# Attention of a two-layer backbone: TensorE order written out, values in groups of six row blocks, VectorE sums three blocks per instruction

## The chip, the cores and the metric

The kernel runs on one core of a Trainium2 chip. The metric is the device time of one execution in microseconds (us). A core has five engines with instruction queues of their own: TensorE (PE; its weight loads are shown apart as PEld), VectorE (DVE), ScalarE (ACT), GpSimd (POOL) and SyncE (SP, here only an issuer of DMAs). Each runs its instructions in the order in which they were put into its queue and waits on semaphores for the others. SBUF is the on-chip memory, PSUM the eight banks into which TensorE writes (a bank holds 512 float32 in each of 128 partitions).

## The reference

Two pre-norm layers over 256 context and 2048 latent tokens, width 1024: multi-head latent attention, then bidirectional gated linear attention. The change is in the softmax attention of the first: 16 heads, 64 plain and 32 rotary numbers a head. Context queries see the 256 context keys, latent queries all 2304.

```python
def one_block(qi):
    s = jnp.einsum('bqhrd,bkhd->bhrqk', qi, k, preferred_element_type=F32) * scale
    p = jax.nn.softmax(s, axis=-1).astype(v.dtype)
    return jnp.einsum('bhrqk,bkhe->bqhre', p, v)
...
oc = attention_blocks(qc, kc, vc)
ox = attention_blocks(qx, jnp.concatenate([kc, kx], axis=1), jnp.concatenate([vc, vx], axis=1))
...
out(o, gate) = (o.reshape(b, n, MLA_WIDTH) * jax.nn.silu(gate)) @ w_out
```

## The kernel before

**Tiling.** The heads are handled in eight pairs. A pair has five *steps*: one of 256 context queries over two key blocks, and four of 512 latent queries over 18 key blocks of 128. A key block of a step is an *item*: 32 × 18 + 8 × 2 = 592, of which 16 are half as wide, 584 in full ones. For an item TensorE makes the scores of both heads (`st`, L603): ten matmuls, five terms in split float32, head 0 in TensorE's row groups of the upper 64 rows and head 1 in the lower 64, which run side by side. ScalarE takes the exponential (`pe`, L605) into one of eight buffers. TensorE multiplies `pe` with the values (`po`, L625, one PSUM bank for a step, four matmuls an item).

**Sums.** The denominator is the sum of the 18 `pe` tiles of a step over blocks and then over keys. VectorE adds the even blocks and the last two into `acc0` (L610 the first pair, L612 the rest), GpSimd the other odd ones into `acc1`; at the end of the step VectorE adds the two (L615), and two pairs of matmuls with ones sum over the keys (L637, `finish`). ScalarE takes the reciprocal by Ln and Exp (L640, L641), GpSimd multiplies the output with its gate (L639) and VectorE with the reciprocal (L643).

**Maxima.** The softmax needs a row maximum, which goes as one more row into the queries of a step. So for each step, ahead of it, TensorE computes approximate scores with queries in the partitions (L484, a *set* of four matmuls: two heads, two terms, 128 queries by 512 keys, the fifth stretch of keys only 256), each head into one of three PSUM banks `pmx`, and VectorE reduces each bank to a maximum (L486). A large step has 4 × 5 = 20 sets, a context step 2. A set needs two of the three banks, so its second bank is one that the set before it used, and is free only when VectorE has reduced that. At the end of a step's maxima (L489 to L495) a small reduce, a transpose on TensorE, a negation and two DMAs put them into the queries. The same three banks serve L637 and the modulation of later layers (L72, L82, L93).

**Order.** A loop over items writes: due sets of maxima (`rate`, about one an item), a modulation part every 20 items, the scores of an item, and after every third block of a step the values of these three (L625). The framework's scheduler then lays each engine's queue out by its own estimate of times; only what is pinned (`keep_in_program_order`) stays as written. In the attention stage nothing on TensorE is pinned.

Of the kernel before, what the change touches and what calls it, by code (L numbers as in the profile page):

```python
# [19 lines left out]
P = 128  # L20
# [44 lines left out]
def modulation_block(k, layer, nb, w, wp, ps, pt, gT, shT, ng, I, sel, condT, gates, gbc_d, bufs, tag="mod_s", bias=None):  # L65


    nc = k.nc
    cs = slice(nb * 512, nb * 512 + 512)
    for i in range(2):  # L70
        for r in range(4):
            nc.tensor.matmul(ps[32 * r:32 * r + 32, :512], condT[:, 4 * i + r, :], w[4 * i + r], start=(i == 0), stop=(i == 1))  # L72
    yield
    if bias is None:
        bias = wp.tile([2, 512], F32, name="mod_b", tag="mod_b", bufs=bufs)
        nc.sync.dma_start(bias, I["ada_b"][layer:layer + 1, cs].to_broadcast([2, 512]))
    m = wp.tile([P, 512], F32, name="mod_s", tag=tag, bufs=bufs)
    nc.scalar.copy(m, ps[:, :512])
    nc.vector.tensor_tensor(m[0:2, :], m[0:2, :], bias, op=ALU.add)
    if nb < 4:  # L80
        for kk in range(4):
            nc.tensor.matmul(pt[:, 2 * kk:2 * kk + 2], m[:, kk * P:kk * P + P], sel[:, 0:2 * P:P], start=True, stop=True)  # L82
        k0 = (nb % 2) * 4
        dst = (shT if nb < 2 else gT)[:, k0:k0 + 4, :]
        src = pt[:, :8].rearrange("p (k c) -> p k c", c=2)
        if nb < 2:
            nc.vector.tensor_copy(dst, src)
        else:
            nc.vector.tensor_scalar(dst, src, 1.0, None, op0=ALU.add)
            nc.vector.tensor_tensor(dst, dst, ng[:, k0:k0 + 4].unsqueeze(2).to_broadcast([P, 4, 2]), op=ALU.mult)  # L90
    else:
        for j in range(gates):
            nc.tensor.matmul(pt, sel[:, j * P:j * P + P], m, start=True, stop=True)  # L93
# [24 lines left out]
def body(ctx, tc, I, out, stop=99, dbg=None):  # L118
# [321 lines left out]
    def load_q(si):  # L440
# [8 lines left out]
        def put():  # L449
            qs = qsp.tile([P, 2, 2, 512], F32R, name="qs", tag="qs")  # L450
# [14 lines left out]

    def maxima():

        for si, (pr, ci) in enumerate(steps):
            c0, n = CHUNKS[ci]
# [6 lines left out]
            for t in range(nq):  # L476
                for b in range(npart):
# [3 lines left out]
                    for i, kk in enumerate((kh, kr[0])):  # L481
                        for j in range(2):
                            js = slice(64 * j, 64 * j + 64)
                            nc.tensor.matmul(ps[j][:, :w], qs[js, 0, i, t * P:t * P + P], kk[js, bs], start=(i == 0), stop=(i == 1))  # L484
                    for j in range(2):
                        nc.vector.reduce_max(mx[:, j * nq + t, b:b + 1], ps[j][:, :w], axis=AX.X)  # L486
                    yield
            mc = qsp.tile([P, 8], F32, name="mc", bufs=2)
            nc.vector.reduce_max(mc[:, :2 * nq], mx[:, :2 * nq, :npart], axis=AX.X)  # L489
            pt = pmp.tile([P, 512], F32, name="pmx")  # L490
            nc.tensor.transpose(pt[:2 * nq, :P], mc[:, :2 * nq], ident)
            mr = qsp.tile([8, P], F32R, name="mr", bufs=2)
            nc.vector.tensor_scalar(mr[:2 * nq, :], pt[:2 * nq, :P], -1.0, None, op0=ALU.mult)
            for j in range(2):
                nc.sync.dma_start(qs[64 * j + 32:64 * j + 33, 1, 1, :n].bitcast(F32), mr[j * nq:j * nq + nq, :].bitcast(F32))  # L495
            yield

    stream = maxima()
    fed, lead, due = 0, 36, 0.0
    with pool("p2q", 2) as sp, pool("ps2q", 5, space=PSUM) as psp:  # L500
# [20 lines left out]
        def feed():  # L521
            nonlocal fed, due
            due += 0.82
            while fed < min(due, lead):
                fed += 1
                next(stream, None)

# [51 lines left out]
    with pool("p3", 2) as sp, pool("ps3", 2, space=PSUM) as psp:  # L579
# [5 lines left out]

        def scores(si, kt, nk):
            pr, ci = steps[si]
            c0, n = CHUNKS[ci]
            kh, kl = kb[pr % 2]
            qs = qss[si]  # L590
            if kt == 0:
                gt = sp.tile([P, 512], F32, name="gt")
                nc.sync.dma_start(gt[:, :n], gate_d[pr, :, c0:c0 + n])
                acc = [sp.tile([P, 2, 512], F32, name=f"acc{e}", tag=f"acc{e}", bufs=1) for e in range(2)]
                live[si] = dict(gt=gt, acc=acc, seen=[[], []], pe={})
            st_ = live[si]
# [3 lines left out]
            for i, (a, s, r, m) in enumerate(terms):  # L600
                for j in range(2):
                    js = slice(64 * j, 64 * j + m)
                    nc.tensor.matmul(st[:, j, :n], a[js, ks], qs[js, s, r, :n], start=(i == 0), stop=(i == len(terms) - 1))  # L603
            pe = sp.tile([P, 2, 512], F32, name="pe", bufs=8)
            nc.scalar.activation(pe[:, :, :n], st[:, :, :n], AF.Exp, scale=SCALE)  # L605
            st_["pe"][kt] = pe
            e = 1 if kt % 2 == 1 and 2 < nk and kt < nk - 2 else 0
            seen, acc, eng = st_["seen"][e], st_["acc"][e], (nc.vector, nc.gpsimd)[e]
            if len(seen) == 1:
                eng.tensor_tensor(acc[:, :, :n], seen[0][:, :, :n], pe[:, :, :n], op=ALU.add)  # L610
            elif len(seen) > 1:
                eng.tensor_tensor(acc[:, :, :n], acc[:, :, :n], pe[:, :, :n], op=ALU.add)  # L612
            seen.append(pe)
            if kt == nk - 1 and st_["seen"][1]:
                nc.vector.tensor_tensor(st_["acc"][0][:, :, :n], st_["acc"][0][:, :, :n], st_["acc"][1][:, :, :n], op=ALU.add)  # L615

        def values(si, kt, nk):
# [5 lines left out]
            po, pe, vt = st_["po"], st_["pe"][kt], vts[pr]  # L623
            for j in range(2):
                nc.tensor.matmul(po[64 * j:64 * j + 64, :n], vt[:, kt, 64 * j:64 * j + 64], pe[:, j, :n], start=(kt == 0), stop=(kt == nk - 1))  # L625
            if kt == nk - 1:
                st_["ob"] = sp.tile([P, 512], F32, name="ob")
                nc.scalar.copy(st_["ob"][:, :n], po[:, :n])

        def finish(si):  # L630
            pr, ci = steps[si]
            c0, n = CHUNKS[ci]
            st_ = live.pop(si)
            acc, ob = st_["acc"][0], st_["ob"]
            pss = pmp.tile([P, 512], F32, name="pmx")
            for j in range(2):
                nc.tensor.matmul(pss[64 * j:64 * j + 64, :n], ones[:, 0:64], acc[:, j, :n], start=True, stop=True)  # L637
            rs = sp.tile([P, 512], F32, name="rs", bufs=1)
            nc.gpsimd.tensor_tensor(ob[:, :n], ob[:, :n], st_["gt"][:, :n], op=ALU.mult)  # L639
            nc.scalar.activation(rs[:, :n], pss[:, :n], AF.Ln)  # L640
            nc.scalar.activation(rs[:, :n], rs[:, :n], AF.Exp, scale=-1.0)  # L641
            yield
            nc.vector.tensor_tensor(ob[:, :n], ob[:, :n], rs[:, :n], op=ALU.mult)  # L643
            (nc.scalar if si == len(steps) - 1 else nc.sync).dma_start(o_d[ci][pr, :, :], ob[:, :n])

        def mods():

            for layer, nb in [(0, 4), (0, 5)] + [(1, nb) for nb in range(6)]:
                w = modulation_load(k, layer, nb, sp)
                yield  # L650
                pm = [pmp.tile([P, 512], F32, name="pmx") for _ in range(2)]
                for _ in modulation_block(k, layer, nb, w, sp, pm[0], pm[1], gT[layer], shT[layer], ng[layer], I, sel, condT, 2 - layer, gbc_d[layer], 1):
                    pass
# [11 lines left out]
        def first_y(oh, ol):  # L665
# [7 lines left out]
            y0 = sp.tile([P, 2, 512], F32, name="y0", tag="pe", bufs=8)  # L673
# [25 lines left out]
        total = sum(21 if ci else 3 for _, ci in steps)  # L699
        rate = total / len(items)  # L700
        fed0 = fed
        done = []
        extra = mods()
        nv = 0
        for i in range(len(items) + 2):
            if i < len(items):
                si, kt, nk = items[i]
                if steps[si][1] == 1 and kt == 6 and steps[si][0] + 1 < NPAIR:
                    tasks += [(load_k, (steps[si][0] + 1, c)) for c in range(len(CHUNKS))]
                    load_v(steps[si][0] + 1)  # L710
                if kt == 0:
                    if si + 3 < len(steps):
                        tasks.insert(sum(f is load_q for f, _ in tasks), (load_q, (si + 3,)))
                if i % 3 == 1:
                    fetch(1)
                while fed < min(lead, fed0 + 0.1 * i) + rate * (i + 1):
                    fed += 1
                    next(stream, None)
                if i > 40 and i % 20 == 10 and i < len(items) - 80:
                    next(extra, None)  # L720
                scores(si, kt, nk)
                if i == len(items) - 70:
                    raw = out_load(0)
                if i == len(items) - 60:
                    out_weights(0, raw)
                if i == len(items) - 40:
                    raw = out_load(1)
                if i == len(items) - 30:
                    o0 = first_o()
            if i >= 2 and (items[i - 2][1] % 3 == 2 or items[i - 2][1] == items[i - 2][2] - 1):  # L730
                for si, kt, nk in items[nv:i - 1]:
                    values(si, kt, nk)
                    if kt == nk - 1:
                        done += [(i + 1 + u, g) for g in [finish(si)] for u in range(2)]
                nv = i - 1
            if i == len(items) + 1:
                out_weights(1, raw)
                first_y(*o0)
            while done and (done[0][0] <= i or i == len(items) + 1):
                next(done.pop(0)[1], None)  # L740
# [744 lines left out]
```

## Time and profile before

| | |
|---|---|
| median of 3 runs | 3941.18 us (3940.01 to 3943.34) |
| the profiled execution | 3936.72 us, span 3934.7 us |
| TensorE busy over the span | 3716.6 us, 94% |
| VectorE, ScalarE, GpSimd busy | 2404.2, 1357.8, 1133.0 us |
| granted TensorE clock, mean of the span | 0.973 of full speed |
| attention stage | 693 to 2559 us of the span |

A matmul of the trace is busy from its start to its modelled end, and consecutive ones overlap, so start-to-start distances tell more than durations. "Idle before" of a group is the time its engine stood still ahead of it, with the instruction that ended it. The granted clock is the share of TensorE's full clock that the throttle gave in a stretch.

### The profile page before, as it was taken

How to read it: one execution, taken by the hardware profiler on the slowest of the kernel's cores; microseconds unless marked ns; L12 is line 12 of the kernel's file. 1: busy time of each engine (PE TensorE's matmuls, PEld its weight loads, DVE VectorE, ACT ScalarE, POOL GpSimd, SP SyncE). 2: the span in 40 equal slices, each digit the busy share in tenths (PEclk: the TensorE clock that was granted, in tenths of full speed). 3: DMA queues.
4: the chain of work that ended last, by engine and by line, in shares of the span. 5: the costliest groups of instructions: out<-in, count | busy, mean ns of one | idle time of the engine just before them, and what ended most of it. 6: DMA issues, size and time to landing. Idle time of an engine off the chain costs nothing.

```text
span 3934.7 us, 59342 instructions
## 1 busy us (share of the span) xinstructions
PE 3716.6 (94%) x24126; PEld 2674.0 (68%) x24126; DVE 2404.2 (61%) x3300; ACT 1357.8 (35%) x1991; POOL 1133.0 (29%) x731
## 2 busy tenths in 40 slices
PE   7999999999999999999999999999999999999799
PEld 5777886555555555555555555577899899999677
DVE  4433335766677666776776677556337777777863
ACT  2322221333333333333333333423224444444441
POOL 3121123334344343443544343455200101000000
PEclk9999999999999999999999999999999999999899
DMA  6210564202102121111101001067775666758442
GB/s 222 82 62 38 204 215 127 83 21 69 49 21 63 42 64 44 45 42 45 53 17 46 22 10 42 9 198 245 246 248 201 205 219 217 235 184 315 153 134 97
DMA packets 280921, 456.01 MB, mean 116 GB/s; under 512 B 23028, under 2 KB 179764, under 8 KB 268680
## 3 DMA queue, kind: packets, MB, share of 16 engines
q1 hardware_dynamic: 216312, 375.21, 28.9%
q10 hardware_dynamic: 64336, 77.02, 5.7%
q8 instruction: 189, 3.10, 0.3%
q14 instruction: 84, 0.69, 0.1%
HBM read 311.27 MB, written 140.71 MB: 115 GB/s over the span
## 4 chain that ended last, share of the span: by engine, by line
PE 68%; issue 8%; DVE 8%; DMA 7%; POOL 4%; ACT 3%; SPq 1%; ACTq 0%; POOLq 0%; DVEq 0%
PE st L603 15%; PE po L625 14%; PE pmx L484 7%; PE pp L903 3%; PE pj L61 3%; PE pj L60 3%; PE pj L62 3%; PE pp L905 3%; PE pp L904 3%; DVE mx L486 2%; DMA wsg<-in_gla_w_in 2%; ACT pe L605 1%; PE pg L1141 1%; PE py L903 1%; DVE acc L612 1%
## 5 line engine op out<-in xcount | busy, mean ns | idle before, releaser
L486 DVE TENSOR_REDUCE mx<-pmx 128x1 f32<-128x512 f32 (+1 forms) x1312 | 767.2, 625 | 403.9 <-PE pmx L484 389.5
L605 ACT ACTIVATE pe<-st 128x1024 f32<-128x1024 f32 (+1 forms) x592 | 600.5, 1014 | 1044.6 <-PE st L603 1042.4
L603 PE MATMUL st<-qs,kbs 64*128 64x512 f32 (+2 forms) x5920 | 913.3, 396 | 0.7 <-DVE t L562 0.6
L603 PEld LDWEIGHTS st<-qs,kbs 64*128 64x128 f32 (+1 forms) x5920 | 630.3, 187 | 130.6 <-issue 20.7
L612 POOL TENSOR_TENSOR acc<-acc,pe 128x1024 f32<-128x1024 f32 x192 | 466.7, 2431 | 619.5 <-ACT pe L605 619.2
L484 PE MATMUL pmx<-kbs,qs 64*128 64x512 f32 (+1 forms) x2624 | 514.4, 400 | 79.0 <-DVE mx L486 66.1
L625 PE MATMUL po<-pe,vt 128*64 128x512 f32 (+1 forms) x2368 | 584.8, 623 | 1.4 <-DMA vt<-v_d 1.4
L484 PEld LDWEIGHTS pmx<-kbs,qs 64*128 64x128 f32 x2624 | 277.9, 187 | 366.1 <-DVE mx L486 191.2
L612 DVE TENSOR_TENSOR acc<-acc,pe 128x1024 f32<-128x1024 f32 x256 | 405.7, 1585 | 141.1 <-ACT pe L605 134.5
L625 PEld LDWEIGHTS po<-pe,vt 128*64 128x64 f32 x2368 | 160.3, 143 | 318.9 <-issue 312.8
L903 PE MATMUL pp<-w,ht 128*128 128x256 f32 x1088 | 318.2, 292 | 0.0
L904 PE MATMUL pp<-w,ht 128*128 128x256 f32 x1088 | 306.0, 281 | 0.0
L905 PE MATMUL pp<-w,ht 128*128 128x256 f32 x1088 | 305.2, 280 | 0.0
L903 PEld LDWEIGHTS pp<-w,ht 128*128 128x128 f32 x1088 | 205.8, 189 | 3.5
L904 PEld LDWEIGHTS pp<-w,ht 128*128 128x128 f32 x1088 | 206.0, 189 | 1.1
L905 PEld LDWEIGHTS pp<-w,ht 128*128 128x128 f32 x1088 | 205.7, 189 | 0.1
L1252 POOL TENSOR_TENSOR orr<-oss,mhalf 128x4 f32<-128x4 f32 x16 | 17.1, 1068 | 651.3 <-DVE oss L1251 651.3
L903 PE MATMUL pp<-ht,w 128*128 128x256 f32 (+1 forms) x616 | 184.3, 300 | 10.1 <-ACT vge L968 6.0
L904 PE MATMUL pp<-ht,w 128*128 128x256 f32 (+1 forms) x616 | 176.4, 286 | 0.0
L905 PE MATMUL pp<-ht,w 128*128 128x256 f32 (+1 forms) x616 | 175.6, 285 | 0.1
L1127 ACT ACTIVATE ex<-df 128x512 f32<-128x512 f32 x192 | 114.2, 632 | 148.3 <-DVE df L1124 132.0
L114 POOL TENSOR_TENSOR rs_r<-rs_v,mhalf 128x1 f32<-128x1 f32 x52 | 29.3, 564 | 379.6 <-DVE rs_v L112 378.1
(371 smaller groups left out, 6238.3 us busy)
## 6 DMA issues: line engine op xcount, KB each, us to landing
ht<-hh_d SPq DMA_DIRECT2D x44, 1024.0 KB
ht<-hl_d SPq DMA_DIRECT2D x44, 1024.0 KB
xt<-in_x SPq DMA_DIRECT2D x32, 512.0 KB
mod_w<-in_ada_w SPq DMA_DIRECT2D x16, 1024.0 KB
v<-gv_d SPq DMA_DIRECT2D x32, 512.0 KB
wsg<-in_gla_w_in SPq DMA_DIRECT2D x66, 192.0 KB
v_d<-vs ACTq DMA_DIRECT2D x18, 512.0 KB
vt<-v_d SPq DMA_DIRECT2D x8, 1152.0 KB
```

The lines of the kernel that those rows point to most:

```text
L60: nc.tensor.matmul(ps, ah, bh, start=(i == 0), stop=False)
L61: nc.tensor.matmul(ps, ah, bl, start=False, stop=False)
L62: nc.tensor.matmul(ps, al, bh, start=False, stop=(i == n - 1))
L484: nc.tensor.matmul(ps[j][:, :w], qs[js, 0, i, t * P:t * P + P], kk[js, bs], start=(i == 0), stop=(i == 1))
L486: nc.vector.reduce_max(mx[:, j * nq + t, b:b + 1], ps[j][:, :w], axis=AX.X)
L603: nc.tensor.matmul(st[:, j, :n], a[js, ks], qs[js, s, r, :n], start=(i == 0), stop=(i == len(terms) - 1))
L605: nc.scalar.activation(pe[:, :, :n], st[:, :, :n], AF.Exp, scale=SCALE)
L612: eng.tensor_tensor(acc[:, :, :n], acc[:, :, :n], pe[:, :, :n], op=ALU.add)
L625: nc.tensor.matmul(po[64 * j:64 * j + 64, :n], vt[:, kt, 64 * j:64 * j + 64], pe[:, j, :n], start=(kt == 0), stop=(kt == nk - 1))
L903: nc.tensor.matmul(ps, ah, bh, start=(i == 0), stop=False)
L904: nc.tensor.matmul(ps, ah, bl, start=False, stop=False)
L905: nc.tensor.matmul(ps, al, bh, start=False, stop=(i == n - 1))
```

## The change

Seven things are changed in the attention stage (lines of the changed kernel):

- The matmuls of scores, maxima, transposes, values and sums are pinned to the order in which the code writes them (`pe_op`).
- The values of up to six blocks stand in one *burst*, after the sixth, twelfth and eighteenth block of a large step and after the second of a small one: 96 bursts of six blocks and 8 of two. In the same burst stand the sums of the step before (`finish`), every third time a part of a modulation block, and the transposes of finished maxima.
- The `pe` tiles are nine slots of one ring.
- Of each six blocks VectorE sums the first three with four `tensor_reduce` instructions (`thirds`, L652): each reads 256 columns of one head from three slots, 768 numbers a partition with the slot as the innermost axis (1024 numbers, 4 KB, apart), and writes 256. GpSimd adds the other three blocks and the two-head tile `part` that comes from them (L643, 11 adds for a large step). VectorE's adds (L610, L612, L615) are gone.
- The output is multiplied with its gate on VectorE straight out of PSUM (`gated`, L669); ScalarE's copy (old L628) and GpSimd's multiply (old L639) are gone; the multiply with the reciprocal goes to GpSimd.
- The stream of maxima starts 30 sets ahead instead of 36, and runs at 1.10 sets an item. The close of a step's maxima is done in bursts.
- Queries of large and small steps have buffers apart, and are loaded two large steps ahead.

```diff
+                            pe_op(nc.tensor.matmul(ps[j][:, :w], qs[js, 0, i, t * P:t * P + P], kk[js, bs], ...))
...
+    def pe_op(i_):
+        return tc.keep_in_program_order(i_) if pinned else i_
...
+        RING = 9
+        ring = sp.tile([P, RING, 2, 512], F32, name="pe", bufs=1)
...
-            pe = sp.tile([P, 2, 512], F32, name="pe", bufs=8)
+            pe = ring[:, slot(si, kt)]
             nc.scalar.activation(pe[:, :, :n], st[:, :, :n], AF.Exp, scale=SCALE)
-            e = 1 if kt % 2 == 1 and 2 < nk and kt < nk - 2 else 0
...
-            if kt == nk - 1 and st_["seen"][1]:
-                nc.vector.tensor_tensor(st_["acc"][0][:, :, :n], st_["acc"][0][:, :, :n], st_["acc"][1][:, :, :n], op=ALU.add)
+            if nk == 2 or kt % 6 > 2:
+                add(si, pe)
...
+                nc.gpsimd.tensor_tensor(st_["acc"][:, :, :n], a[:, :, :n], part[:, :, :n], op=ALU.add)
+        def thirds(si, kt):
+            part = sp.tile([P, 2, 512], F32, name="part", bufs=1)
+            s0 = slot(si, kt)
+            for j in range(2):
+                for c in (0, 256):
+                    src = ring[:, s0:s0 + 3, j, c:c + 256].rearrange("p s c -> p c s")
+                    nc.vector.tensor_reduce(part[:, j, c:c + 256], src, axis=AX.X, op=ALU.add)
+            add(si, part)
...
+        def gated(si):
+            nc.vector.tensor_tensor(st_["ob"][:, :n], st_["po"][:, :n], st_["gt"][:, :n], op=ALU.mult)
...
+        rate = (sum(20 if ci else 2 for _, ci in steps) - fed) / (len(items) - 24)
+        pinned = True
+        def burst(i, end=False):
+            group = items[nv:i]
...
+            for c in cl:
+                next(c)
+            for si, kt, nk in group:
+                values(si, kt, nk)
+            while done:
+                finish(done.pop(0))
+            if nb > 4 and nb % 3 == 0 and i < len(items) - 70:
+                next(extra, None)
+            for c in cl:
+                next(c)
+            for si, kt, nk in group:
+                if nk > 2 and kt % 6 == 0:
+                    thirds(si, kt)
+            if kt == nk - 1:
+                gated(si)
+                done.append(si)
...
+            scores(si, kt, nk)
+            if i and (items[i - 1][1] % 6 == 5 or items[i - 1][1] == items[i - 1][2] - 1):
+                burst(i)
```

TensorE's queue before, from one group of values in the middle of the attention stage on (`kbs_3830` and `kbs_3831` are the two buffers that hold the keys, `64x512 x6` the values of three blocks in six rows of the listing):

```order
L625 MATMUL po<-pe,vt 64x512 x6
L484 MATMUL pmx<-kbs_3830,qs 128x512 x2
L484 MATMUL pmx<-kbs_3831,qs 128x512 x2
L484 MATMUL pmx<-kbs_3830,qs 128x512
L484 MATMUL pmx<-kbs_3831,qs 128x512
L603 MATMUL st<-qs,kbs_3830 128x512
L484 MATMUL pmx<-kbs_3830,qs 128x512
L484 MATMUL pmx<-kbs_3831,qs 128x512
L603 MATMUL st<-qs,kbs_3830 128x512 x5
L603 MATMUL st<-qs,kbs_3831 128x512 x4
```

The second set of maxima stands split: one head of it right behind the first set, on the third bank, the other after a first single matmul of the scores.

TensorE's queue of the changed kernel, from the values of six blocks on, in a large step:

```order
L663 MATMUL po<-pe,vt 64x512 x12
L491 MATMUL pmx<-kbs_3831,qs 128x512 x4
L626 MATMUL st<-qs,kbs_3830 128x512 x6
L626 MATMUL st<-qs,kbs_3831 128x512 x4
L491 MATMUL pmx<-kbs_3831,qs 128x512 x4
L626 MATMUL st<-qs,kbs_3830 128x512 x6
L626 MATMUL st<-qs,kbs_3831 128x512 x4
L491 MATMUL pmx<-kbs_3831,qs 128x256 x4
L626 MATMUL st<-qs,kbs_3830 128x512 x6
L626 MATMUL st<-qs,kbs_3831 128x512 x4
L491 MATMUL pmx<-kbs_3831,qs 128x512 x4
L626 MATMUL st<-qs,kbs_3830 128x512 x6
```

Now whole sets of maxima and whole scores alternate, and six blocks of values stand together.

VectorE's queue before, around the end of a step (`acc_14959` and `acc_14960` are the two accumulators of that step, `acc_15440` the first one of the next):

```order
L486 TENSOR_REDUCE mx<-pmx 128x1 x2
L612 TENSOR_TENSOR acc_14959<-acc_14959,pe 128x1024
L486 TENSOR_REDUCE mx<-pmx 128x1 x3
L612 TENSOR_TENSOR acc_14959<-acc_14959,pe 128x1024
L486 TENSOR_REDUCE mx<-pmx 128x1
L615 TENSOR_TENSOR acc_14959<-acc_14959,acc_14960 128x1024
L486 TENSOR_REDUCE mx<-pmx 128x1 x6
L610 TENSOR_TENSOR acc_15440<-pe 128x2x256
```

Single adds stand between the reduces that free the banks.

VectorE's queue of the changed kernel, in the same stretch as TensorE's rows above (`mx` are the reduces of the maxima, `part` the four instructions over three slots):

```order
L669 TENSOR_TENSOR ob<-po,gt 128x512
L493 TENSOR_REDUCE mx<-pmx 128x1 x6
L652 TENSOR_REDUCE part<-pe 128x256 x3
L493 TENSOR_REDUCE mx<-pmx 128x1 x2
L652 TENSOR_REDUCE part<-pe 128x256
L493 TENSOR_REDUCE mx<-pmx 128x1 x12
L652 TENSOR_REDUCE part<-pe 128x256 x3
```

The code writes the four behind the values; in the queue three of them stand behind the six reduces of the first three sets after the values, and the fourth behind the two of the next set. All 96 groups stand among such reduces.

## Rows read from the trace of the kernel before

**Rows 1.** Windows: stretch, length, busy (count) PE, PEld, DVE, ACT, POOL, clock, DMA share, GB/s.

```profile
693.00:2559.00 1866.00, 1759.32 (x11138) 996.77 (x11140) 1276.01 (x1707) 679.48 (x731) 788.84 (x399) 0.97 0.13 41
```

**Rows 2.** Groups by line, attention stage: busy, mean ns, idle before and what ended it.

```profile
L603 PE MATMUL st<-qs,kbs 64*128 64x512 f32 (+2 forms) x5920 | 913.3, 396 | 0.7 <-DVE t L562 0.6
...
L625 PE MATMUL po<-pe,vt 128*64 128x512 f32 (+1 forms) x2368 | 584.8, 623 | 1.4 <-DMA vt<-v_d 1.4
L484 PE MATMUL pmx<-kbs,qs 64*128 64x512 f32 (+1 forms) x2486 | 484.1, 398 | 70.3 <-DVE mx L486 65.8
L612 POOL TENSOR_TENSOR acc<-acc,pe 128x1024 f32<-128x1024 f32 x192 | 466.7, 2431 | 619.5 <-ACT pe L605 619.2
L612 DVE TENSOR_TENSOR acc<-acc,pe 128x1024 f32<-128x1024 f32 x256 | 405.7, 1585 | 141.1 <-ACT pe L605 134.5
...
L615 DVE TENSOR_TENSOR acc<-acc,acc 128x1024 f32<-128x1024 f32 x31 | 69.1, 2228 | 0.1
...
L637 PE MATMUL pmx<-acc,ones 128*64 128x512 f32 (+1 forms) x156 | 38.7, 574 | 0.0
...
L491 PE MATMUL pmx<-ident,mc 128*8 128x128 f32 (+1 forms) x38 | 10.4, 274 | 28.9 <-ACT pe L605 15.3 <-DVE mc L489 13.7
```

**Rows 3.** Timeline of TensorE, a quiet stretch: start, length, engine, line, operation, count.

```profile
1317.61 2.80 PE L625 MATMUL po<-pe,vt 128*64 128x512 f32 x12
1320.34 0.73 PE L484 MATMUL pmx<-kbs,qs 64*128 64x512 f32 x4
1320.91 1.32 PE L603 MATMUL st<-qs,kbs 64*128 64x512 f32 x10
1322.06 0.63 PE L484 MATMUL pmx<-kbs,qs 64*128 64x512 f32 x4
1322.53 1.33 PE L603 MATMUL st<-qs,kbs 64*128 64x512 f32 x10
1323.68 0.65 PE L484 MATMUL pmx<-kbs,qs 64*128 64x512 f32 x4
1324.14 1.33 PE L603 MATMUL st<-qs,kbs 64*128 64x512 f32 x10
1325.41 2.80 PE L625 MATMUL po<-pe,vt 128*64 128x512 f32 x12
```

**Rows 4.** Timeline of VectorE and ScalarE in the same stretch.

```profile
1321.10 1.29 DVE L486 TENSOR_REDUCE mx<-pmx 128x1 f32<-128x512 f32 x2 [1.50 <-PE pmx L484]
1322.27 1.03 ACT L605 ACTIVATE pe<-st 128x1024 f32<-128x1024 f32 x1 [3.52 <-PE st L603]
```

**Rows 5.** Timeline of VectorE and TensorE around the end of a step.

```profile
1110.77 2.79 DVE L615 TENSOR_TENSOR acc<-acc,acc 128x1024 f32<-128x1024 f32 x1
...
1113.49 1.99 DVE L486 TENSOR_REDUCE mx<-pmx 128x1 f32<-128x512 f32 x4
...
1114.22 0.58 PE L484 MATMUL pmx<-kbs,qs 64*128 64x256 f32 x1 [2.36 <-DVE mx L486]
```

**Rows 6.** Windows around the same place, columns as in the first group.

```profile
1107.10:1110.50 3.40, 3.32 (x25) 2.36 (x22) 3.06 (x5) 1.02 (x1) 2.45 (x2) 1.00 0.00 0
1110.50:1113.90 3.40, 1.36 (x9) 0.59 (x7) 3.40 (x3) 1.03 (x1) 1.98 (x1) 1.00 0.02 4
1113.90:1117.30 3.40, 3.08 (x12) 1.72 (x14) 1.57 (x4) 0.91 (x1) 0.00 (x0) 0.50 0.48 155
1117.30:1120.70 3.40, 3.40 (x12) 0.78 (x8) 0.00 (x0) 0.11 (x1) 0.00 (x0) 0.50 0.01 2
```

**Rows 7.** Groups by line and shape, VectorE, whole span.

```profile
L486 DVE TENSOR_REDUCE mx<-pmx 128x1 f32<-128x512 f32 x1024 | 661.4, 684 | 355.8 <-PE pmx L484 348.2 <-PE st L603 6.5
...
L486 DVE TENSOR_REDUCE mx<-pmx 128x1 f32<-128x256 f32 x288 | 108.4, 417 | 48.1 <-PE pmx L484 41.3
...
L610 DVE TENSOR_TENSOR acc<-pe 128x1024 f32<-128x1024 f32 x32 | 39.2, 1225 | 35.9 <-ACT pe L605 35.9
L1117 DVE TENSOR_TENSOR ex<-b 128x512 f32<-128x512 f32 x16 | 10.9, 682 | 0.0
```

More of the change, by code (lines that the diff above doesn't have):

```diff
@@ L79, in modulation_block @@
     nc.vector.tensor_tensor(m[0:2, :], m[0:2, :], bias, op=ALU.add)
+    bank = pt if callable(pt) else lambda pt=pt: pt
+    if callable(pt):
+        yield
     if nb < 4:
+        pt = bank()
         for kk in range(4):
@@ L92, in modulation_block @@
         for j in range(gates):
+            pt = bank()
             nc.tensor.matmul(pt, sel[:, j * P:j * P + P], m, start=True, stop=True)
@@ L526, in feed @@
                 next(stream, None)
+                while closes:
+                    for _ in closes.pop():
+                        pass
         for ci, (c0, n) in enumerate(CHUNKS):
@@ L592, in scores @@
                 gt = sp.tile([P, 512], F32, name="gt")
[L593 to L596, printed above, removed]
+                nc.sync.dma_start(gt[:, :n], gate_d[pr, :, CHUNKS[ci][0]:CHUNKS[ci][0] + n])
+                live[si] = dict(gt=gt, acc=sp.tile([P, 2, 512], F32, name="acc"), seen=[])
             st = psp.tile([P, 2, 512], F32, name="st", bufs=2)
@@ L650, in mods @@
                 yield
-                pm = [pmp.tile([P, 512], F32, name="pmx") for _ in range(2)]
-                for _ in modulation_block(k, layer, nb, w, sp, pm[0], pm[1], gT[layer], shT[layer], ng[layer], I, sel, condT, 2 - layer, gbc_d[layer], 1):
-                    pass
+                bank = lambda: pmp.tile([P, 512], F32, name="pmx")
+                for i, _ in enumerate(modulation_block(k, layer, nb, w, sp, bank(), bank, gT[layer], shT[layer], ng[layer], I, sel, condT, 2 - layer, gbc_d[layer], 1)):
+                    if i:
+                        yield
                 yield
@@ L698, in body @@
         load_v(0)
-        total = sum(21 if ci else 3 for _, ci in steps)
-        rate = total / len(items)
+        rate = (sum(20 if ci else 2 for _, ci in steps) - fed) / (len(items) - 24)
         fed0 = fed
[L702 to L740, printed above, removed]
@@ new lines, in body @@
+        pinned = True
+        done, extra, nv, nb = [], mods(), 0, 0
+        def burst(i, end=False):
+            nonlocal nv, nb
+            group = items[nv:i]
+            nv = i
+            nb += 1
+            cl = list(closes)
+            closes.clear()
+            for c in cl:
[11 more added lines that the diff above has]
+                    thirds(si, kt)
+            si, kt, nk = group[-1]
+            if kt == nk - 1:
+                gated(si)
+                done.append(si)
+            for c in cl:
+                next(c, None)
@@ new lines, in body @@
+        for i, (si, kt, nk) in enumerate(items):
+            if steps[si][1] == 1 and kt == 6 and steps[si][0] + 1 < NPAIR:
+                tasks += [(load_k, (steps[si][0] + 1, c)) for c in range(len(CHUNKS))]
+                load_v(steps[si][0] + 1)
+            if kt == 0 and steps[si][1]:
+                large = [s for s in range(si, len(steps)) if steps[s][1]][1:3]
+                for s in range(large[0] + 1, large[1] + 1) if len(large) == 2 else ():
+                    tasks.insert(sum(f is load_q for f, _ in tasks), (load_q, (s,)))
+            if i % 3 == 1:
+                fetch(1)
+            while fed < fed0 + rate * (i + 1):
+                fed += 1
+                next(stream, None)
+            scores(si, kt, nk)
+            if i == len(items) - 70:
+                raw = out_load(0)
+            if i == len(items) - 60:
+                out_weights(0, raw)
+            if i == len(items) - 40:
+                raw = out_load(1)
+            if i == len(items) - 30:
+                o0 = first_o()
+            if i and (items[i - 1][1] % 6 == 5 or items[i - 1][1] == items[i - 1][2] - 1):
+                burst(i)
@@ L741, in body @@
+        burst(len(items))
+        out_weights(1, raw)
+        for si in done:
+            finish(si)
+        first_y(*o0)
     att_q.close()
```

75 lines of the change are left out of this document (41 added, 34 removed).

## The prediction

> **What bounds the kernel now.** I read the attention stage by itself first, since everything that moves lies in it. The window of the stage shows TensorE busy 1759 of 1866 us, with the clock at 0.97, and VectorE busy 1276, with ScalarE and GpSimd far lower [rows 1]. The groups by line then show for whom TensorE stands: nearly all of its idle time stands ahead of the maxima and is ended by VectorE's reduce `mx` [rows 2]. So TensorE sets the length, and VectorE decides when it may go on.
>
> What an undisturbed matmul group costs is read from starts in the timeline [rows 3]: three blocks of values 2.73 us (0.91 a block); a set of maxima 0.47, but 0.57 behind values (+0.11); a score 1.15, but 1.27 ahead of values (+0.12). A burst thus costs 0.23 in switches. Summed over the stage: 584 full score items × 1.15 = 672; values 584 × 0.91 = 531; 2486 / 4 = 621 sets of maxima [rows 2], a fifth of them half as wide, 0.46 and 0.23 = 255; the small lines (row sums 38.7, transposes 10.4 [rows 2], and the modulation) 75; 200 bursts × 0.23 = 46; the 39 row sums and 38 transposes, each with a switch of its own, 77 × 0.23 = 18. That is 1597. The other 269 us are TensorE's idle time, 1866 − 1759 = 107; the clock, 0.03 × 1866 = 56; and 106 left over, which I put to broken pairs: where a set of maxima is split around a lone score matmul, as the first piece of order shows, the two heads no longer run side by side.
>
> [...]
>
> **What the change takes away.** 96 fewer bursts × 0.23 = 22 us. Row sums and transposes stand behind values in the same burst: 18. The pinned order keeps sets and scores whole: the 106. L615 goes, and transposes no longer wait in front of scores: with them the 107 idle and the 56 of the clock, as far as no new wait comes. Five more sets lie in the stage (30 ahead instead of 36, 656 in all): +2. Without new waits the stage would take 1866 − 22 − 18 − 269 + 2 = 1559.
>
> **What it adds.** First, work that I cost at nothing because other work hides it. GpSimd has 11 adds in a large step, 11 × 2.43 = 27 us [rows 2], in a step of at least 1559 / 32.4 = 48 us (584 / 18 = 32.4 large steps), and their sum is needed only in the burst after the step's last. The slot of a block is written again nine items later, after the burst and the sum that read it; if the GpSimd add came late there, the exponential, which now has 1.03 us in some 2.3 an item [rows 4], would wait. The multiply `gated` costs about one 512-wide pass, 0.7 us, 40 times on VectorE; it holds `po` until then, but the next values come some 14 us later (six scores and six or seven sets). ScalarE's copy goes; ScalarE doesn't bound. VectorE as a whole gets lighter: 406 + 69 us of adds [rows 2] against 384 reduces.
>
> A reduce over three slots (768 numbers) isn't in the trace. By the maxima's reduces, 684 ns for 512 and 417 for 256 [rows 7], a number costs 1.04 ns and an instruction 0.15 us, so 0.95; back to back (two in 1.29 where they are 0.684 alone [rows 4, 7]) 0.92. Bounds: 0.46 if 768 numbers go at the pace of L610, 2048 in 1.225 us [rows 7]; 1.73 if GpSimd's reading beside it stretches it as L615 is stretched against L610, 2228 / 1225 = 1.82 [rows 2, 7]. I take 0.92, the row of the same instruction. [...]
>
> **The new wait.** It is in the order, not in the load. In the last piece of VectorE's order three of the four reduces over slots stand ahead of the reduces of the fourth set after a burst, the fourth ahead of those of the fifth. Count from the first set after the values, with 0.57 / 0.47 for a set, 1.15 for a score, a set's reduces beginning 0.76 after it and 0.645 each [rows 3, 4]. Sets start at 0, 1.72, 3.33 and 4.95; the score behind the fourth ends at 6.56. VectorE ends the third set's reduces at 4.09 + 1.29 = 5.38, three slot reduces at 8.14, the fourth set's first reduce at 8.78. The three banks rotate, so the fifth set's second half needs the bank that this one frees: wanted at about 6.8, it starts at 8.8, and TensorE stands 2.0 us. Queued behind are the whole fifth set, its score and everything up to the next burst, since the order is pinned. VectorE then ends the fourth slot reduce at 10.35 and the fifth set's first reduce at 11.0; the sixth set wants that bank at 10.4: another 0.6. Together 2.6 a burst, about 0.5 less where the third set is the half-wide one; I take 2.5 × 96 bursts = 240 us. With the bounds 0.46 and 1.73 of the slot reduce the same count gives 0.6 and 5.7 a burst: 60 and 547. Small shifts in the phase leave 150 to 310 by the row that I chose.
>
> **The clock.** Each of these 96 waits is of the kind behind which the clock fell [rows 5, 6], though a little shorter (2.0 against 2.36). At the 1.8 us that an event cost before: 96 × 1.8 = 173. Lower bound 0, if the shorter wait doesn't drop it; upper bound 2.8 × 96 = 270, if the two scores and the set up to the next values all go at half speed.
>
> **Sum.** 1559 + 240 + 173 = 1972 us for the stage, 106 more than 1866. The profiled execution took 3936.7 (span 3934.7 and 2.0 around it), so 4043; the median of the runs shown is 4.5 above that execution, so I forecast 4047 us, 2.7% slower. Waits and clock together decide at (1866 − 1559) / 96 = 3.2 us a burst; I have 4.3.
>
> **The rivals.**
> A. The waits come, but the clock holds. For it: the new waits are shorter than the one in [rows 5]; against it: there, one of 2.36 cost two whole stretches [rows 6]. 1559 + 240 is 67 less than 1866: 3874. Chance 0.22.
> A2. The waits hardly come, because the slot reduces run faster (0.46) or VectorE is early enough to have them done before the fourth set. For it: VectorE has 1276 of 1866 us busy, so there is slack on average [rows 1]; against it: its place in the queue is fixed, behind the third set's reduces. 1559 + 0 to 60: about 3634 to 3694. Chance 0.08.
> B. The slot reduce is dear, 1.7 us, because of its reading. Its numbers are read with 4 KB between neighbours. The nearest row is L1117, with one number between neighbours, which takes 682 ns for 512, as a dense reduce does [rows 7], but such a small distance doesn't test 4 KB. Then the waits are 5.7 a burst, 547, and with the clock's 173 the stage takes 2279: 4354; with half the extra cost 4200. Chance 0.10. [...]
> C. The change doesn't do what it says on TensorE: pairs stay broken for another reason than the order. Then up to 106 us come on top: up to 4153, within my range, so it gets no chance of its own.
>
> **How the numbers follow.** The forecast's case (waits of 150 to 310 us, the clock between 50 and 270) has 0.60, with its own range 3960 to 4130. A has 0.22, A2 0.08, B 0.10. The 80% range takes in A and half of B: 3850 to 4230. A measurement of this kernel tells 0.2% (8 us) from no change. Faster: A and A2, 0.30; slower: B and nearly all of the forecast's case, 0.65; same: where waits and clock come to the 3.2 us that balance, 0.05.
>
> **What will show it.** Right: in the changed kernel TensorE's idle time ahead of the maxima (L491) is ended by `mx`, about 2.0 and then 0.6 us in each of 96 bursts; the slot reduces (L652) have a mean near 0.93; six blocks of values stand in one row of about 5.5 us; scores keep 1.15; the clock of the stage is near 0.91 (173 / 1972 lost). Wrong: a clock that stays at 0.97 or higher with the waits there (A); idle time under 80 us in all (A2); L652 at 1.4 or more (B); scores and maxima summing to more than 672 and 257 at full clock (C).

## The result and the profile after

The changed kernel takes 3989.8 us (3982.7 to 3993.3, four runs) against 3942.3: ratio 1.0119, 95% interval 1.0101 to 1.0136. It is slower, as forecast, by 47.5 us instead of 106. The profiled execution has a span of 3988.3 us.

Windows of the changed kernel: the attention stage, then two pairs of stretches in one large step (columns as in [rows 1]).

```profile
692.00:2606.50 1914.50, 1700.97 (x11153) 1042.04 (x11153) 1137.89 (x1770) 662.01 (x694) 1054.03 (x532) 0.96 0.13 40
...
1499.40:1502.80 3.40, 2.59 (x24) 1.86 (x22) 3.40 (x6) 2.05 (x2) 0.64 (x1) 1.00 0.00 0
1502.80:1506.20 3.40, 2.47 (x21) 1.62 (x17) 3.40 (x6) 1.02 (x1) 3.02 (x2) 1.00 0.00 0
1518.50:1521.90 3.40, 1.77 (x13) 1.14 (x11) 3.40 (x5) 1.07 (x2) 3.14 (x2) 0.95 0.00 0
1521.90:1525.30 3.40, 3.04 (x16) 1.90 (x14) 2.74 (x5) 1.02 (x1) 1.85 (x2) 0.54 0.02 5
```

The stage is 48 us longer than in [rows 1], with TensorE busy 58 us less and VectorE 138 less: what it gained in work, it more than lost in waiting, 213 us of idle time against 107. The groups by line of that stage say where:

```profile
L626 PE MATMUL st<-qs,kbs 64*128 64x512 f32 (+2 forms) x5920 | 897.6, 409 | 3.1 <-ACT pe L628 3.0
...
L663 PE MATMUL po<-pe,vt 128*64 128x512 f32 (+1 forms) x2368 | 525.6, 592 | 6.4 <-DMA vt<-v_d 6.4
L491 PE MATMUL pmx<-kbs,qs 64*128 64x512 f32 (+1 forms) x2499 | 523.6, 414 | 205.7 <-DVE mx L493 203.3 <-DVE mr L508 0.3
L652 DVE TENSOR_REDUCE part<-pe 128x256 f32<-128x768 f32 x384 | 380.4, 1029 | 34.5 <-ACT pe L628 34.3
```

Against [rows 2] the idle time ahead of the maxima has gone from 70 to 206 us, nearly all of it ended by VectorE's reduce (66 and 203). The timeline of TensorE shows three such waits, two short ones ahead of a burst, then a long one after the fourth set behind that burst (start, length, line, count, idle before):

```profile
1501.78 0.72 PE L491 MATMUL pmx<-kbs,qs 64*128 64x512 f32 x3 [0.81 <-DVE mx L493]
...
1504.61 0.72 PE L491 MATMUL pmx<-kbs,qs 64*128 64x512 f32 x3 [0.93 <-DVE mx L493]
...
1517.31 0.64 PE L491 MATMUL pmx<-kbs,qs 64*128 64x512 f32 x4
1517.78 1.34 PE L626 MATMUL st<-qs,kbs 64*128 64x512 f32 x10
1518.95 0.40 PE L491 MATMUL pmx<-kbs,qs 64*128 64x512 f32 x1
1520.98 0.50 PE L491 MATMUL pmx<-kbs,qs 64*128 64x512 f32 x2 [1.63 <-DVE mx L493]
```

and VectorE's, what it did around the long one:

```profile
1514.95 2.15 DVE L493 TENSOR_REDUCE mx<-pmx 128x1 f32<-128x512 f32 x4 [0.33 <-PE pmx L491]
1517.30 1.04 DVE L652 TENSOR_REDUCE part<-pe 128x256 f32<-128x768 f32 x1 [0.20 <-ACT pe L628]
...
1518.36 1.96 DVE L652 TENSOR_REDUCE part<-pe 128x256 f32<-128x768 f32 x2
1520.25 1.27 DVE L493 TENSOR_REDUCE mx<-pmx 128x1 f32<-128x512 f32 x2
1521.44 1.02 DVE L652 TENSOR_REDUCE part<-pe 128x256 f32<-128x768 f32 x1
```

Behind the burst, the fifth set has issued one matmul; the next waits for a bank whose reduce stands behind three slot reduces. It starts 2.0 us late, of which TensorE is idle 1.63. Behind this wait the clock is at half speed for one stretch (0.54 in the window from 1521.90); the pair of windows from 1499.40 holds two waits of 0.81 and 0.93 us, behind a split of two and two slot reduces, at a clock of 1.00. Of the 96 groups of four slot reduces 71 ran as three and one in the trace, 18 as two and two, 3 in three pieces and 4 whole, without such a wait.

The stretches at half speed in the stage sum to 171 us, so they cost about 85. The account of the stage is 213 idle + 85 clock + 1616 of work, against 107 + 56 + 1703 before. (Half the length of a stretch at half speed is put down to the clock, also where TensorE stood idle in it; that is 5 of the 171 us here.)

### The profile page after: what moved, and what is told of

It is laid out like the page before. It is cut to its first block, busy times and chain, and to the rows that moved or that the text cites. A ratio compares the mean times of both kernels' runs of the same rounds, so it can differ in the third digit from the quotient of the medians.

```text
span 3988.3 us, 59297 instructions
## 1 busy us (share of the span) xinstructions
PE 3658.7 (92%) x24126; PEld 2721.2 (68%) x24126; DVE 2258.8 (57%) x3356; ACT 1335.6 (33%) x1951; POOL 1402.2 (35%) x867
## 4 chain that ended last, share of the span: by engine, by line
PE 64%; DVE 17%; DMA 7%; issue 6%; POOL 2%; ACT 2%; SPq 1%; ACTq 0%; POOLq 0%; DVEq 0%
PE po L663 13%; PE st L626 12%; DVE part L652 8%; PE pmx L491 7%; DVE mx L493 5%; PE pj L60 4%; PE pj L61 4%; PE pj L62 4%; PE pp L964 2%; PE pp L965 2%; PE pp L966 2%; PE py L61 1%; PE py L60 1%; PE py L62 1%; DMA wsg<-in_gla_w_in 1%
## 5 line engine op out<-in xcount | busy, mean ns | idle before, releaser
L628 ACT ACTIVATE pe<-st 128x1024 f32<-128x1024 f32 (+1 forms) x592 | 600.0, 1014 | 1034.7 <-PE st L626 983.3
L626 PE MATMUL st<-qs,kbs 64*128 64x512 f32 (+2 forms) x5920 | 897.6, 409 | 3.1 <-ACT pe L628 3.0
L491 PE MATMUL pmx<-kbs,qs 64*128 64x512 f32 (+1 forms) x2624 | 551.0, 414 | 213.5 <-DVE mx L493 203.3
L626 PEld LDWEIGHTS st<-qs,kbs 64*128 64x128 f32 (+1 forms) x5920 | 669.5, 198 | 110.1 <-ACT pe L628 7.8
L643 POOL TENSOR_TENSOR acc<-acc,pe 128x1024 f32<-128x1024 f32 x224 | 532.2, 2376 | 449.6 <-ACT pe L628 416.4
L491 PEld LDWEIGHTS pmx<-kbs,qs 64*128 64x128 f32 x2624 | 311.2, 197 | 401.9 <-DVE mx L493 301.0
L663 PE MATMUL po<-pe,vt 128*64 128x512 f32 (+1 forms) x2368 | 525.6, 592 | 6.4 <-DMA vt<-v_d 6.4
L652 DVE TENSOR_REDUCE part<-pe 128x256 f32<-128x768 f32 x384 | 380.4, 1029 | 34.5 <-ACT pe L628 34.3
L643 POOL TENSOR_TENSOR acc<-acc,part 128x1024 f32<-128x1024 f32 x96 | 229.2, 2388 | 7.5
```

Source lines behind the costliest of these rows:

```text
L491: pe_op(nc.tensor.matmul(ps[j][:, :w], qs[js, 0, i, t * P:t * P + P], kk[js, bs], start=(i == 0), stop=(i == 1)))
L626: pe_op(nc.tensor.matmul(st[:, j, :n], a[js, ks], qs[js, s, r, :n], start=(i == 0), stop=(i == len(terms) - 1)))
L643: nc.gpsimd.tensor_tensor(st_["acc"][:, :, :n], a[:, :, :n], part[:, :, :n], op=ALU.add)
L652: nc.vector.tensor_reduce(part[:, j, c:c + 256], src, axis=AX.X, op=ALU.add)
L663: pe_op(nc.tensor.matmul(po[64 * j:64 * j + 64, :n], vt[:, kt, 64 * j:64 * j + 64], pe[:, j, :n], start=(kt == 0), stop=(kt == nk - 1)))
```

## Experiments

**VectorE's order.** The maxima's reduces and the slot reduces are chained in the order of the code; nothing else changes.

```diff
+    def ve_op(i_):
+        if pinned:
+            if ve_last:
+                tc.add_manual_dep(i_.ins, ve_last[0].name, ... NoSync ...)
+            ve_last[:] = [i_.ins]
+        return i_
...
-                        nc.vector.reduce_max(mx[:, j * nq + t, b:b + 1], ps[j][:, :w], axis=AX.X)
+                        ve_op(nc.vector.reduce_max(mx[:, j * nq + t, b:b + 1], ps[j][:, :w], axis=AX.X))
...
-                    nc.vector.tensor_reduce(part[:, j, c:c + 256], src, axis=AX.X, op=ALU.add)
+                    ve_op(nc.vector.tensor_reduce(part[:, j, c:c + 256], src, axis=AX.X, op=ALU.add))
```

> Edit: the changed kernel with VectorE's order chained as written, so that the four slot reduces of a burst stand behind the reduces of the last set ahead of the values, and run beside the values. Theory (the place in VectorE's queue makes the waits, and these drop the clock): four reduces at 0.948 are 3.8 us, with one or two maxima reduces left over they fit beside the 5.3 us of values; idle time ahead of the maxima falls from 204 us to under 40, the clock of the attention stage rises to 0.99, and the time goes to 3634 plus at most 60: 3630 to 3700. Rival 1 (pinned order, ring and six blocks at a time cost the time themselves): the waits move to the first sets behind the values or to the scores, time 3900 or more. Rival 2 (the slot reduces cost by what they read or load on VectorE): time 3800 to 3950.

Measured 3721.3 us, ratio to before 0.9444 (0.943 to 0.9459). VectorE's timeline in a burst whose values run on TensorE from 1424.25 to 1429.62:

```profile
1421.67 2.18 DVE L493 TENSOR_REDUCE mx<-pmx 128x1 f32<-128x512 f32 x4 [0.34 <-PE pmx L491]
1423.77 3.86 DVE L661 TENSOR_REDUCE part<-pe 128x256 f32<-128x768 f32 x4
1429.67 0.69 DVE L678 TENSOR_TENSOR ob<-po,gt 128x512 f32<-128x512 f32 x1 [2.04 <-PE po L672]
1430.31 1.29 DVE L493 TENSOR_REDUCE mx<-pmx 128x1 f32<-128x512 f32 x2
```

The four slot reduces lie whole beside the values, with 2.04 us to spare. The groups and the window of that kernel's stage:

```profile
L491 PE MATMUL pmx<-kbs,qs 64*128 64x512 f32 (+1 forms) x2499 | 443.2, 385 | 37.7 <-DVE mx L493 36.2 <-DVE mr L508 0.3
...
L661 DVE TENSOR_REDUCE part<-pe 128x256 f32<-128x768 f32 x384 | 370.3, 1026 | 25.6 <-ACT pe L637 25.6
```

```profile
692.00:2343.00 1651.00, 1590.94 (x11153) 999.82 (x11151) 1155.61 (x1770) 662.17 (x694) 1057.40 (x532) 0.99 0.15 47
```

Same instructions, same TensorE order, 268 us less. The place in VectorE's queue is shown to be what made the changed kernel slow; both rivals fall. The time is 21 us over the upper end expected. Idle time ahead of the maxima is 38, under the 40 expected: 21 of it are 37 waits of 0.5 to 0.7 us, put down to places where two sets stand back to back, and 8 a single wait. What I had left out is 22 us of other idle time (1651 − 1591 − 38), 14 of it ahead of the row sums.

**Without the slot reduces.** In the changed kernel GpSimd adds a constant tile in place of their result; the denominators lack three of six blocks.

```diff
+        cpart = sp.tile([P, 2, 512], F32, name="cpart", bufs=1)
+        nc.vector.memset(cpart, 1.0)
...
-            part = sp.tile([P, 2, 512], F32, name="part", bufs=1)
...
-            add(si, part)
+            add(si, cpart)
```

> Edit: the changed kernel without the slot reduces; GpSimd adds a constant tile in place of their result, so three of six blocks are missing from the denominators. Theory (the reduces cost only where they stand): the floor of the new TensorE order, within 25 us of the 3721 of the chained order. Rival (the reduces still cost by load on VectorE or by reading): 3670 or less.

Measured 3712.5 us in one run; the stage's window:

```profile
689.50:2325.50 1636.00, 1589.15 (x11153) 1001.68 (x11153) 798.18 (x1387) 662.70 (x694) 1056.39 (x532) 0.99 0.15 47
```

Against the first experiment VectorE's load falls by 357 us and the time by 9, about as much as the runs of one kernel differ. Beside the values the slot reduces are all but free.

**All four behind the third set.** The chain again, but `thirds` is called after the third set behind the values.

```diff
                 if nk > 2 and kt % 6 == 0:
-                    thirds(si, kt)
+                    late.append([3, si, kt])
...
                 next(stream, None)
+                if late:
+                    late[0][0] -= 1
+                    if late[0][0] == 0:
+                        thirds(*late.pop(0)[1:])
...
```

> Edit: the changed kernel with VectorE's order chained, but all four slot reduces put right behind the reduces of the third set after the values, without the split of three and one. By hand the fifth set's second half is 3.0 us late and the sixth none: idle about 2.6 us in one piece a burst, 250 us in all against 204. What a wait costs in clock is disputed: by the price that the changed kernel shows for its waits (176 us at half speed for 96 bursts, 0.92 us each) the time is about 4040; if the clock falls more often and for longer behind one long wait than behind two short ones, as the price before had it (1.8 us or more each), about 4120 to 4150.

Measured 4192.4 us in one run. Window and groups of its stage:

```profile
691.00:2813.50 2122.50, 1776.98 (x11153) 1108.89 (x11153) 1142.24 (x1770) 657.37 (x694) 1054.41 (x532) 0.89 0.12 36
```

```profile
L491 PE MATMUL pmx<-kbs,qs 64*128 64x512 f32 (+1 forms) x2499 | 525.6, 431 | 256.2 <-DVE mx L493 254.9 <-DVE mr L508 0.3
...
L687 PE MATMUL pmx<-acc,ones 128*64 128x512 f32 (+1 forms) x156 | 43.3, 637 | 83.7 <-POOL acc L652 83.7
```

The waits for maxima came as counted (256 against 250). The row sums wait 84 us more behind GpSimd's late adds, in seven waits, each in the burst of a small step, which stands only two items after the burst before it; nobody had expected them. Without these 84 us some 4108 are left, just under the second expectation and well over the first. The clock was at half speed for 461 us, but TensorE stood idle in 90 of these, so it lost about 185 and not 230. In the 84 bursts with a wait for maxima of 1.95 us or more and no other wait (mostly one of 2.75) the clock lost 2.1 us a burst, 2.3 times the changed kernel's 0.89 for 1.25 times the idle time ahead of the maxima. That price is the second expectation's, 1.8 or more.

**Two and two.** The same with two slot reduces behind the second set and two behind the third (the countdown above is [2] and [1], each call does one head).

> Edit: the changed kernel with VectorE's order chained, two of the four slot reduces behind the second set after the values and two behind the third. By hand two waits a burst, 1.1 and 1.6 us late (about 0.7 and 1.2 idle), 2.7 in all against 3.0 in one piece when all four stand behind the third set (4192 us, clock of the stage 0.89). Theory (the clock is lost by long single waits, not by the sum): nearly as much lateness, but under 40 us at the clock, so about 3975 and a clock of the stage of 0.98. Rival (each wait, or the idle time in sum, has its price in clock): 85 to 200 us of it, 4020 to 4150, clock 0.90 to 0.96.

Measured 4058.7 us in one run, 84 over the theory's number and within the rival's, but with a wait that neither had counted. Groups and window of its stage:

```profile
L491 PE MATMUL pmx<-kbs,qs 64*128 64x512 f32 (+1 forms) x2499 | 518.8, 412 | 198.2 <-DVE mx L493 196.8 <-DVE mr L508 0.3
...
L695 PE MATMUL pmx<-acc,ones 128*64 128x512 f32 (+1 forms) x156 | 43.2, 636 | 89.1 <-POOL acc L652 89.1
```

```profile
689.00:2680.50 1991.50, 1698.32 (x11153) 1024.67 (x11153) 1136.60 (x1771) 657.28 (x694) 1054.49 (x532) 0.95 0.13 39
```

The row sums again wait for GpSimd, 89 us in seven waits of up to 16, with the clock at half speed around them; that part of the run says nothing on the question, and without the 89 us some 3970 are left, close to the theory's 3975. Sorting the bursts by their longest single wait for the maxima answers it. Over the changed kernel, this one, the one before and the first, without bursts that hold another wait: longest wait 0.25 to 1.25 us, 124 bursts, half speed in 12; 1.25 to 1.95 in the changed kernel, 62 bursts, half speed in 30, and 0.88 us lost a burst on average; 1.95 and more, 110 bursts, half speed in 92, with 2.1 us lost a burst in the kernel with all four behind the third set. In 64 bursts of this kernel with short waits alone the idle time summed to 2.1 us as in those 62, and the clock lost 0.3 us a burst. So the long single wait is dear, not the sum; but the short ones aren't quite free, and the theory's 40 us was a little low: the bursts of this kernel without a wait for row sums lost 46.

**Before with TensorE pinned.**

```diff
-                            nc.tensor.matmul(ps[j][:, :w], ...)
+                            pe_op(nc.tensor.matmul(ps[j][:, :w], ...))
...
-                    nc.tensor.matmul(st[:, j, :n], ...)
+                    pe_op(nc.tensor.matmul(st[:, j, :n], ...))
...
-                nc.tensor.matmul(po[64 * j:64 * j + 64, :n], ...)
+                pe_op(nc.tensor.matmul(po[64 * j:64 * j + 64, :n], ...))
...
```

> Edit: the kernel before, with the matmuls of maxima, scores and values alone kept in written order (values of three blocks, sums as before). It measures the 106 us put to broken pairs by themselves. If that term is right and L615's waits stay (107 idle, 56 clock): 3941 - 106 = 3835. If the unpinned order hid waits for VectorE, which the pinned one must sit out: 3941 or more.

Measured 3978.4 us, ratio 1.0094 (1.0069 to 1.0119): slower. Window and group of its stage:

```profile
694.50:2605.00 1910.50, 1736.64 (x11139) 982.23 (x11138) 1281.46 (x1704) 680.18 (x732) 785.00 (x398) 0.95 0.13 40
```

```profile
L484 PE MATMUL pmx<-kbs,qs 64*128 64x512 f32 (+1 forms) x2483 | 453.9, 405 | 125.2 <-DVE mx L486 123.0 <-ACT rs L645 0.3
```

The pairs do mend: idle time and clock set aside (174 and 90), the stage's work is 1646 us against 1703. But idle time grows by 67 and the clock's loss by 34: that fits a loose order which had let TensorE do other work while VectorE was at a long add. The second expectation holds.

**The changed kernel with the sums of before.**

```diff
-            if nk == 2 or kt % 6 > 2:
-                add(si, pe)
+            st_ = live[si]
+            e = 1 if kt % 2 == 1 and 2 < nk and kt < nk - 2 else 0
+            seen, acc, eng = st_["sums"][e], st_["accs"][e], (nc.vector, nc.gpsimd)[e]
...
-                if nk > 2 and kt % 6 == 0:
-                    thirds(si, kt)
+                pass
```

> Edit: the changed kernel with the sums of the kernel before (VectorE adds ten blocks and the join of both accumulators, GpSimd seven), all else as changed: written TensorE order, values of six, ring, output gated on VectorE. Theory (the join makes one long wait a step, as before): 3634 + 32 x (2.4 idle + 0.4 + 1.8 of clock) = 147 and some 50 us for single adds between the maxima: 3780 to 3880. If the single adds hold the fixed order as much as they did in the kernel before with TensorE's order pinned (3978): 3930 or more, and the gain of the chained order is then the slot reduces' own.

Measured 3919.8 us, ratio 0.9938 (0.9917 to 0.9959): 40 over the range that I had given, near the other expectation. Groups of its stage:

```profile
L491 PE MATMUL pmx<-kbs,qs 64*128 64x512 f32 (+1 forms) x2499 | 518.6, 411 | 151.8 <-DVE mx L493 148.2 <-DVE mr L508 0.3
...
L636 DVE TENSOR_TENSOR acc<-acc,pe 128x1024 f32<-128x1024 f32 x256 | 485.6, 1897 | 27.6 <-ACT pe L629 24.1
```

VectorE's single adds take 1897 ns here against 1585 in [rows 2], and the fixed order has to sit out what they hold up. The change without its new sums is worth 23 us; the new sums, with the slot reduces where they were queued, cost 70, and with the slot reduces at the right place they gain 199.

**A better version.** From the first experiment's kernel: at most one set ahead of a score, and the one left over in the middle of the values.

```diff
-            for si, kt, nk in group:
+            for u, (si, kt, nk) in enumerate(group):
+                if u == 3:
+                    thirds(*group[0][:2])
+                    if fed + 1 <= fed0 + rate * (i + 2):
+                        fed += 1
+                        next(stream, None)
                 values(si, kt, nk)
...
-            for si, kt, nk in group:
-                if nk > 2 and kt % 6 == 0:
-                    thirds(si, kt)
...
-            while fed < fed0 + rate * (i + 1):
+            if fed < fed0 + rate * (i + 1):
```

> Edit: the kernel with VectorE's order chained (3721), with at most one set of maxima ahead of each score, and the set that is left over put in the middle of the six blocks of values. In that kernel two sets back to back wait 0.55 us and break a set (0.4) 37 times or more; in the middle of the values a set costs two switches, 0.23. Expected: 37 x 0.7 = 26 us less, 3695. If VectorE, with the four slot reduces ahead of that set's reduces, comes late for the first sets behind the values: 3721 or more.

Measured 3693.2 us, ratio 0.9368 (0.9349 to 0.9386). Its waits for maxima are nearly gone:

```profile
L491 PE MATMUL pmx<-kbs,qs 64*128 64x512 f32 (+1 forms) x2504 | 410.1, 385 | 9.3 <-DVE mx L493 6.0 <-DVE mr L508 2.6
```

**What the distance costs.** The four reduces of the first experiment's kernel read dense numbers. Their result is left unused, GpSimd adds a constant tile, and `ob` has one buffer.

```diff
-                    src = ring[:, s0:s0 + 3, j, c:c + 256].rearrange("p s c -> p c s")
+                    src = ring[:, s0 + (2 * j + c // 256) % 3].rearrange("p j c -> p (j c)")[:, 0:768].rearrange("p (c s) -> p c s", s=3)
...
```

> Edit: the kernel with VectorE's order chained (3721), with its four slot reduces reading 768 numbers side by side in one slot instead of three slots 4 KB apart; their result is left unused, GpSimd adds a constant tile, and ob has one buffer. It measures what the distance costs. Rival B (distance is dear): one reduce alone goes from 1.03 us to 0.75 or less. By the maxima's reduces (0.15 + 768 x 1.04 ns): 0.95, and 0.92 back to back against 0.94 to 0.95 now; then at most 0.08 us of the 1.03 is the distance. If nothing hangs on it: 1.03 again. The time of the kernel stays at 3721 within 20 us.

Measured 3799.0 us in one run. Groups of its stage:

```profile
L663 DVE TENSOR_REDUCE part<-pe 128x256 f32<-128x768 f32 x384 | 364.9, 950 | 49.2 <-ACT pe L639 26.9 <-DVE part L663 0.9
...
L680 DVE TENSOR_TENSOR ob<-po,gt 128x512 f32<-128x512 f32 (+1 forms) x40 | 25.5, 637 | 126.0 <-PE po L674 48.4 <-DMA o_d<-ob 37.9 <-issue 25.3
```

A dense reduce takes 950 ns, the 0.95 worked out from the maxima's rows, and one over 4 KB 1026 to 1029: the distance costs 0.08 us, 8%. Those that stand right behind a reduce of the maxima, 92 in each kernel, take 942 and 1026 ns, the same 0.08. The kernel's time came out 78 us too high: with one `ob` VectorE stands 11 to 13 us ahead of `gated` six times, 38 us of it for the output's DMA by the trace, and TensorE 10.5 to 12.2 us behind each of these. That price of the one buffer was not foreseen; the duration of a single reduce doesn't hang on it.

## Why the prediction was wrong

The sign and the mechanism were right; one term was mis-sized, and it made the forecast more than twice the change.

- **The floor, 1559 us.** The chained order and the kernel without slot reduces leave 1572 and 1574 us when their idle time (60 and 47) and clock (19 and 15) are taken off. Right within 15.
- **The slot reduce, 0.92 us.** 0.948 from start to start back to back, 1.03 alone. Rival B's 1.7 falls: of its reason the traces show the sign, 1.03 with 4 KB between neighbours against 0.95 with none, and no more. The bound of 1.73, for a slot reduce stretched by GpSimd's work beside it, falls too: in the changed kernel slot reduces with GpSimd busy over 90% of their time take 1028 ns (171 of them), and with it nearly idle 1031 (141). VectorE's adds of two tiles are stretched: in the kernel with the sums of before those of L636 take 1220 ns (54) with GpSimd idle, 2196 (13) with it busy over 90% of their time, and 2113 in the 180 between a tenth and 90%. The kernel before has the same two kinds: of its 31 adds L615, 11 with GpSimd idle take 1.21 us and 20 beside its work 2.79. The 2228 ns of [rows 2], from which the bound of 1.73 was worked out, is a mean of the two; L610, its measure of an undisturbed add (1225 ns [rows 7]), adds two tiles as well, and GpSimd is idle beside nearly all 32.
- **The waits, 240 us.** 206 idle, and 44 more of work than the floor's 1572, which I put to sets that a wait breaks in two: 250. Right in sum. Of the 44, 40 lie in the maxima: from start to start, without idle time and at full clock, they take 340 us here and 300 in the chained order, while the scores take 699 and 694. So pairs do stay broken, which is rival C's sign; that the waits break them fits these numbers and no run shows it by itself.
- **The clock, 173 us: the step that failed.** "At the 1.8 us that an event cost before: 96 × 1.8 = 173." It cost 85; the stage's clock is 0.96, not 0.91. No run shows 1.8 us as the price of an event: the number is the stage's 56 us shared among 31 adds L615 that are not alike. Eleven are short, with no such wait behind them. Thirteen leave TensorE idle for 2.1 to 2.4 us, and behind twelve of these the clock fell, 34 us in all, 2.6 each. Behind six more the wait is 1.45 us, and the clock never fell; the rest of the 56 stands behind other waits. One of the six, in the kernel before (TensorE, then windows with columns as in [rows 1]):

```profile
929.97 0.50 PE L484 MATMUL pmx<-kbs,qs 64*128 64x256 f32 x2 [1.45 <-DVE mx L486]
```

```profile
929.40:932.80 3.40, 2.83 (x12) 1.05 (x12) 1.77 (x4) 0.00 (x0) 2.40 (x4) 1.00 0.10 32
932.80:936.20 3.40, 3.40 (x21) 1.75 (x22) 1.36 (x3) 1.72 (x3) 3.40 (x3) 1.00 0.51 87
```

The new waits I had put at "2.0 against 2.36", but 2.0 was how late the second half of a set starts; one matmul of the set still runs in it, so the idle time is 1.63 in the timeline above and mostly 1.5 to 1.9. That lies between the waits that dropped the clock before and those that didn't. And 18 groups were split two and two, mostly with waits of about 0.8 and 0.9 us instead of one long one. Of the waits of 1.25 to 1.95 us about half dropped the clock, mostly for one stretch and not two. The experiment with 2.75 us in one piece lost 2.1 us a burst: the price depends steeply on the length of a single wait, and I carried a mean over unlike waits to another length.

1572 + 44 + 213 + 85 = 1914. The forecast had 1972: 88 too much for the clock, 30 too little for the rest. In this term rival A (the clock holds) was as far off as the forecast, since the clock did half of what I said; in the time its 3874 was twice as far off as 4047. A mean of both, 3960, would have been nearer than either.

- **What I cost at nothing.** GpSimd's 11 adds and the ring held in the changed kernel (row sums waited 5 us or less). That they hold only as long as VectorE hands over its sums early is shown by the two kernels with late slot reduces, where row sums wait 84 and 89 us, all of it in the bursts of small steps.
- **The 106 us of broken pairs.** Pinning alone mends 57 of them and loses 101 to waits and clock; the rest of the 106 no run shows apart. It took VectorE's order as well: the stage's work goes from 1703 to 1572 us there, 131, where the forecast took off 106 + 22 + 18 and put on 2.

What stays open is why the scheduler set the slot reduces among the maxima; and why waits of one length drop the clock in some places and not in others: the price of the short ones is known only as 12 in 124 bursts, that of 1.25 to 1.95 us as 30 in 62.

## What to carry to other kernels

When one engine's order is pinned, read the queue of the engine that frees its buffers as well: the same four instructions cost 277 us a run at one place (3989.8 against 3712.5 without them) and 9 at another, beside a long run of TensorE that needs nothing from VectorE. Price a wait twice, as idle time and as clock, and take the clock's price only from waits of the same idle length, not from a mean over unlike waits and not from how late an instruction starts.

## What the runs showed of the hardware

A reduce over three places 4 KB apart costs 8% more than over neighbours (1.03 against 0.95 us), far from double. Waits of TensorE that sum to the same idle time, 2.1 us a burst, lost 0.3 us a burst at the clock in pieces below 1.25 us and 0.88 in bursts with a piece of 1.25 to 1.95; bursts with a piece of 1.95 and more lost 2.0. In the kernel before, thirteen waits of 2.1 to 2.4 us lost 2.6 us each, and six of 1.45 none. VectorE's adds of two tiles take 1.22 us with GpSimd idle and, as means of two kernels, 1.6 to 2.2 beside its work; the reduce over three slots takes 1.03 either way.
